# Inverting 16 by 16 triangles in 8 by 8 halves, and issuing their block loads from two engines

## The chip, the cores and the metric

The kernel runs on one core of a Trainium2 chip. The metric is device time in microseconds (us) of one execution; lower is better. Five engines work side by side, each through its own list of instructions in order: TensorE (PE: matmuls and transposes), VectorE (DVE), ScalarE (ACT), GpSimd (POOL) and SyncE (SP, which here only issues DMAs). They wait for one another through semaphores.

## The reference

One gated-DeltaNet layer, then one MoBA attention layer, on 256 tokens of width 1024, float32, 8 heads of 128. What matters here is the first layer's delta rule, in chunks of 64 tokens:

```python
lower = jnp.where(strict, jnp.einsum('nbhid,nbhjd->nbhij', k_beta, k) * decay, 0.0)
a_mat = jnp.eye(C, dtype=jnp.float32) + lower
w = lax.linalg.triangular_solve(a_mat, k_beta * jnp.exp(gc)[..., None],
                                left_side=True, lower=True, unit_diagonal=True)
u = lax.linalg.triangular_solve(a_mat, v * beta[..., None],
                                left_side=True, lower=True, unit_diagonal=True)
```

## The kernel before, in words

The kernel does the same with chunks of 128 tokens (two, t = 0 and 1) and inverts the unit triangular matrix of each head and chunk. The 8 heads make two groups of four; a group has 8 matrices of 128 by 128 (4 heads, 2 chunks). `inverse(grp)` handles one group:

- The 64 diagonal blocks of 16 by 16 (8 matrices, 8 blocks) are fetched from a DRAM copy `md` into tile `inv`, one block in each of 64 partitions. Tile part `mb` is the block (transposed), `t16` the inverse that grows in it, `tr` the pair (inverse, transposed inverse).
- Substitution (lines 742 to 749): 15 steps, each an outer product and an addition over what is left of the block, so 30 instructions. Group 0 does them on POOL, group 1 on DVE (`INVERSE`, line 48).
- SP writes `tr` to the DRAM scratch `td` (752), waits until it has landed, and issues eight small DMAs (755 to 757) that bring it back as blocks on the diagonal of tile `TC`, which is part of tile TR of the group (TR0, TR1). This is the block layout of the change's title.
- PE then doubles the blocks: `ps_x`, `ps_y` (16 to 32), `ps_x5`, `ps_y5` (to 64), `ps_x6`, `ps_y6` (to 128), with copies on DVE and ACT between. `solve` applies the inverse: `ps_s1`, `ps_s2`, `ps_s3`, and `read_out` (`ps_o`, `ps_og`) makes the operand o of the output projection (o0 and o1 for the two groups).

PE is kept busy meanwhile by projections: heads' v (`ps_v`), the gate z (`ps_z`), and the first half of the output projection (`ps_y<-hi,o`, 128x512), which needs o0 alone; its second half needs o1. A v head goes through ACT (copy with a scale), DVE (three steps of a convolution on tile `cv`), ACT again (`cv<-cv`, the silu) and back to PE as a transpose (`ps_vt`). Weights arrive by SP's DMAs as `raw`, are cut into `hi` (ACT) and `lo` (DVE), and a `raw` buffer is loaded again after its `lo`.

The order on every engine is fixed when the program is built. `Clock` estimates when each instruction would run, and `Pipeline` puts a chain's next step after a PE step when the estimate says that its operands are there. In these estimates a DMA issue takes its engine 60 ns (line 172), on SP as on ACT, and a POOL operation on `inv` takes 480 ns and 1.2 ns for each element (199). `ps_x` is put no earlier than 1500 ns after the estimated landing of TC (766). A change in one chain so moves instructions on all engines. Nearly all instructions bear line 220, where they are recorded, so the views are read by tile.

Of the kernel before, what the change touches and what calls it, by code (L numbers as in the profile page):

```python
# [20 lines left out]
ALU = mybir.AluOpType  # L21
# [205 lines left out]
class Pipeline:  # L227
# [12 lines left out]
    def at(self, e):  # L240
        return self.clock.t.get(self.ENGINES[e], START)
# [66 lines left out]
def body(ctx, tc, x, xt, cst_in, w0, wp, a_ln_g, a_ln_b, b_ln_g, b_ln_b, out):  # L308
    ctx.enter_context(tc.manual_schedule())
    nc = Clock(tc.nc)  # L310
# [358 lines left out]
    def gs_head(h):  # L669
# [41 lines left out]
        if n_md[h // 4] == 4:  # L711
            pipe.add(inverse(h // 4), R_INV)
# [8 lines left out]
    def inverse(grp):  # L721
        inv = act.tile([64, 4, 16, 16], F32, tag="ag" if grp == 0 else "ab", name=f"inv{grp}")
        mb, tr, prod = inv[:, 0], inv[:, 1:3], inv[:, 3]
# [7 lines left out]
        TC = T[:, 1024:1536].rearrange("p (w q c) -> p w q c", w=2, q=8)  # L731
        T64 = T[0:64, 1536:2048].rearrange("p (q c) -> p q c", q=8)
        t16 = tr[:, 0]
# [4 lines left out]
                                        ap=[[16 * (P + 1), 64]] + list(blk.ap)))  # L738
        eng, e = INVERSE[grp]
        eng = getattr(nc, eng)  # L740
        yield e, [inv]
        for j in range(15):

            m, r = 15 - j, j + 1
            eng.tensor_mul(prod[:, 0:m, 0:r], mb[:, j, r:16].unsqueeze(2).to_broadcast([64, m, r]),
                           t16[:, j, 0:r].unsqueeze(1).to_broadcast([64, m, r]))
            eng.tensor_add(t16[:, r:16, 0:r], t16[:, r:16, 0:r], prod[:, 0:m, 0:r])
            if j in (4, 9):
                yield e, [t16]
        eng.tensor_copy(tr[:, 1], t16.rearrange("p a b -> p b a"))  # L750
        yield "t", [inv]
        nc.sync.dma_start(td[grp].rearrange("w q b r c -> (q b) w (r c)"),
                          tr.rearrange("p w r c -> p w (r c)"))
        yield "t", [td[grp]]
        for b in range(8):
            nc.sync.dma_start(TC.rearrange("p w q c -> p (w q) c")[16 * b:16 * b + 16, :, 16 * (b % 2):16 * (b % 2) + 16],
                              td[grp].rearrange("w q b r c -> b r (w q) c")[b])

        def ms(q):
# [500 lines left out]
```

## Time and profile before

| | |
|---|---|
| time, median of 3 runs | 301.84 us (301.78 to 303.9) |
| the profiled execution's own time | 302.44 us |
| its span, first to last instruction | 300.5 us |
| PE busy | 289.7 us, 96% |
| DVE, ACT, POOL busy | 210.2, 161.6, 51.2 us |
| mean granted TensorE clock | 0.993 |

The span is what the instructions cover; 1.94 us of the profiled execution lie around it. A window's row gives each engine's busy time in it, so 10 us less PE's figure is what PE stood idle there. A timeline row merges like instructions that follow one another (x10) and gives the idle time of the engine before them, if any, with what ended it.

### The profile page before, as it was taken

What the parts mean: (1) busy time and instruction counts of PE and PEld (TensorE: products, weight loads), DVE (VectorE), ACT (ScalarE), POOL (GpSimd) and SP (SyncE); (2) the same over time, 40 slices, a digit from 0 to 9 for tenths busy, and PEclk for the clock granted to TensorE, in tenths of its full rate; (3) what the DMA queues carried; (4) which work ended last, traced back from release to release, by engine and by line L of the source; (5) the groups of instructions that cost most, each with busy time, mean ns of one, the idle gap of its engine ahead of it and who ended that gap; (6) DMA issues with size and microseconds to landing.
All of it is one profiled execution on the core that took longest, in us unless ns stands there. A gap on an engine that the chain in (4) does not pass through costs nothing.

```text
span 300.5 us, 6569 instructions
## 1 busy us (share of the span) xinstructions
PE 289.7 (96%) x2598; PEld 266.7 (89%) x2598; DVE 210.2 (70%) x477; ACT 161.6 (54%) x329; POOL 51.2 (17%) x92
## 2 busy tenths in 40 slices
PE   8998999999999999999989999999999999999990
PEld 7898989989999989996878888899999999998890
DVE  0699479999999587687449893865655565763545
ACT  2588986635866552865352525775655558561000
POOL 8002310265884300110020010000000000000101
PEclk9999999999999999999999999999999999999997
DMA  6986505659576711336629055895444447400012
GB/s 224 377 278 223 177 17 176 214 165 316 189 258 182 235 61 29 93 127 209 201 108 328 2 179 172 256 313 199 143 129 153 144 143 273 142 0 2 0 70 71
DMA packets 19934, 49.43 MB, mean 164 GB/s; under 512 B 6304, under 2 KB 7968, under 8 KB 19904
## 3 DMA queue, kind: packets, MB, share of 16 engines
q1 hardware_dynamic: 18592, 46.73, 47.3%
q0 software_dynamic: 448, 1.18, 1.4%
q10 hardware_dynamic: 864, 1.11, 1.1%
q8 instruction: 20, 0.33, 0.5%
q14 instruction: 10, 0.08, 0.1%
HBM read 46.65 MB, written 2.36 MB: 163 GB/s over the span
## 4 chain that ended last, share of the span: by engine, by line
PE 77%; ACT 7%; DMA 5%; issue 5%; DVE 4%; ACTq 0%; POOL 0%; POOLq 0%; DVEq 0%; SPq 0%
PE ps_bkq L220 15%; PE ps_y L220 11%; PE ps_kq L220 9%; PE ps_v L220 8%; PE ps_bv L220 7%; PE ps_bz L220 7%; PE ps_z L220 5%; PE ps_g L220 4%; DMA raw<-in_wp_dram 4%; ACT ME L220 3%; DMA zraw<-in_w_dram 2%; PE ps_o L220 2%; PE ps_ot L220 2%; PE ps_sc L220 2%; PE ps_s L220 1%
## 5 line engine op out<-in xcount | busy, mean ns | idle before, releaser
L220 DVE TENSOR_TENSOR lo<-raw,hi 128x1024 fp32r<-128x1024 f32 (+1 forms) x79 | 94.6, 1207 | 10.1 <-ACT hi L220 9.9
L220 ACT CAST hi<-raw 128x1024 fp32r<-128x1024 f32 (+1 forms) x79 | 80.3, 1037 | 12.6 <-DMA raw<-in_wp_dram 6.5
L220 PE MATMUL ps_y<-hi,o 128*128 128x512 f32 (+1 forms) x144 | 43.5, 374 | 0.8 <-ACT o L220 0.7
L220 PE MATMUL ps_bkq<-x1h,hi 128*128 128x256 f32 x128 | 38.0, 297 | 0.0
L220 PE MATMUL ps_kq<-xh,hi 128*128 128x256 f32 x128 | 36.6, 286 | 0.0
L220 PE MATMUL ps_kq<-xh,lo 128*128 128x256 f32 x128 | 35.7, 279 | 0.0
L220 PE MATMUL ps_kq<-xl,hi 128*128 128x256 f32 x128 | 35.6, 278 | 0.0
L220 PE MATMUL ps_bkq<-x1l,hi 128*128 128x256 f32 x128 | 35.6, 278 | 0.0
L220 PE MATMUL ps_bkq<-x1h,lo 128*128 128x256 f32 x128 | 35.5, 278 | 0.0
L220 PEld LDWEIGHTS ps_y<-hi,o 128*128 128x128 f32 x144 | 25.9, 188 | 5.9 <-ACT o L220 1.2
L220 POOL TENSOR_TENSOR mv<-mv,nhalf 128x1 f32<-128x1 f32 x4 | 3.8, 951 | 135.0 <-DVE mv L220 135.0
L220 PE MATMUL ps_y<-lo,o 128*128 128x512 f32 (+1 forms) x72 | 26.3, 366 | 0.0
L220 DVE SCALAR_TENSOR_TENSOR cv<-ps_kq,cst_sb,cv 128x255 f32<-128x255 f32 (+2 forms) x48 | 21.5, 470 | 4.8 <-ACT cv L220 4.6
L220 PEld LDWEIGHTS ps_bkq<-x1h,hi 128*128 128x128 f32 x128 | 24.1, 189 | 0.2
L220 PEld LDWEIGHTS ps_bkq<-x1l,hi 128*128 128x128 f32 x128 | 24.1, 188 | 0.2
L220 PEld LDWEIGHTS ps_kq<-xh,hi 128*128 128x128 f32 x128 | 24.3, 190 | 0.0
L220 PEld LDWEIGHTS ps_kq<-xh,lo 128*128 128x128 f32 x128 | 24.0, 188 | 0.1
L220 PEld LDWEIGHTS ps_kq<-xl,hi 128*128 128x128 f32 x128 | 24.1, 188 | 0.0
L220 PEld LDWEIGHTS ps_bkq<-x1h,lo 128*128 128x128 f32 x128 | 24.1, 188 | 0.0
L220 PE MATMUL ps_v<-xh,hi 128*128 128x256 f32 x64 | 18.7, 292 | 0.0
L220 PE MATMUL ps_bz<-x1h,hi 128*128 128x256 f32 x64 | 18.0, 282 | 0.0
L220 PE MATMUL ps_v<-xl,hi 128*128 128x256 f32 x64 | 17.9, 280 | 0.0
(177 smaller groups left out, 676.6 us busy)
## 6 DMA issues: line engine op xcount, KB each, us to landing
raw<-in_wp_dram SPq DMA_DIRECT2D x77, 512.0 KB, 4.2
md<-ME POOLq DMA_DIRECT2D x8, 128.0 KB, 2.6
late<-in_x_dram SPq DMA_DIRECT2D x1, 1024.0 KB, 4.9
zraw<-in_w_dram ACTq DMA_DIRECT2D x4, 136.0 KB, 4.3
zraw<-in_w_dram ACTq DMA_DIRECT2D x2, 272.0 KB, 4.8
x_sb<-in_xt_dram SPq DMA_DIRECT2D x4, 128.0 KB, 4.1
x_sb<-in_xt_dram SPq DMA_DIRECT2D x2, 256.0 KB, 5.0
raw<-in_wp_dram SPq DMA_DIRECT2D x2, 256.0 KB, 4.1
```

What stands on the lines that cost most here:

```text
L220: r = f(*args, **kw)
```

## The change

The 16 by 16 inverse is made of two 8 by 8 ones. Seven steps of substitution run on both 8-blocks at once (14 instructions of 14 to 32 elements in each partition, where there were 30 of 15 to 64). One merge follows, of two products of three 8 by 8 matrices: each product is one multiplication of 512 elements and a sum over 8, on DVE one reduction, on POOL three additions (256, 128 and 64 elements). The multiplications and reductions are separated by points at which the planner may put other work. Of the eight loads of the block layout, SP issues four and ACT four, ACT's after the same wait for `td`.

```diff
-        for j in range(15):
-            m, r = 15 - j, j + 1
-            eng.tensor_mul(prod[:, 0:m, 0:r], mb[:, j, r:16].unsqueeze(2).to_broadcast([64, m, r]),
-                           t16[:, j, 0:r].unsqueeze(1).to_broadcast([64, m, r]))
-            eng.tensor_add(t16[:, r:16, 0:r], t16[:, r:16, 0:r], prod[:, 0:m, 0:r])
-            if j in (4, 9):
-                yield e, [t16]
+        wide = tr[:, 1]
+        for j in range(7):
+            m, r = 7 - j, j + 1
+            pv = at(wide, 0, 0, (m * r, 2), (r, m), (1, r))
+            tv = at(t16, r, 0, (136, 2), (16, m), (1, r))
+            eng.tensor_mul(pv, at(mb, j, r, (136, 2), (1, m), (0, r)), at(t16, j, 0, (136, 2), (0, m), (1, r)))
+            eng.tensor_add(tv, tv, pv)
+            if j == 3:
                 yield e, [t16]
+        p8 = at(wide, 0, 0, (64, 8), (8, 8), (1, 8))
+        for out, left, right in (...):
+            eng.tensor_mul(p8, left, right)
+            yield e, [inv]
+            if e == "v":
+                eng.tensor_reduce(out, p8, axis=mybir.AxisListType.X, op=ALU.add)
+            else:
+                for w in (4, 2, 1):
...
+                    eng.tensor_add(d, x0, x1)
+            yield e, [inv]
         eng.tensor_copy(tr[:, 1], t16.rearrange("p a b -> p b a"))
...
         for b in range(8):
-            nc.sync.dma_start(TC...[16 * b:16 * b + 16, ...],
+            (nc.scalar if b % 2 else nc.sync).dma_start(TC...[16 * b:16 * b + 16, ...],
```

From the first moved instruction (late in the k and q heads) to the end of the first layer the order differs; from the second layer on PE's order is as before. Three places are shown.

First, ACT while group 0's inverse comes back (cv_1257 before and cv_1260 now are the same head). Before:

```order
L220 ACTIVATE cv_1316<-ps_v_1253,cst_sb_82 128x256
L220 CAST hi31_1319<-raw31_1171 128x1024
L220 ACTIVATE cv_1257<-cv_1257 128x256
L220 ACTIVATE cv_1371<-ps_v_1311,cst_sb_82 128x256
L220 CAST hi32_1373<-raw32_1195 128x1024
```

Now:

```order
L220 ACTIVATE cv_1311<-ps_v_1247,cst_sb_82 128x256
L220 CAST hi31_1314<-raw31_1154 128x1024
L220 DMA TR0_845<-td_174 16x16x16 x4
L220 ACTIVATE cv_1260<-cv_1260 128x256
L220 ACTIVATE cv_1366<-ps_v_1307,cst_sb_82 128x256
L220 CAST hi32_1368<-raw32_1182 128x1024
```

Four DMA issues now stand ahead of the silu of this head; PE's transpose of it comes three projection matmuls earlier than before, and group 0's `ps_x` six.

Second, ACT while group 0 is solved (Z is the solve's result, jk2 the squares of its read-out). Before:

```order
L220 CAST hi36_1706<-raw36_1394 128x1024
L220 ACTIVATE cv_1757<-ps_v_1700,cst_sb_82 128x256
L220 COPY Z_1771<-ps_s1_1773 128x512
L220 ACTIVATE cv_1625<-cv_1625 128x256
L220 ACTIVATE jk2_1820,sso_177<-ps_o_1805 128x128
```

Now:

```order
L220 ACTIVATE W_175<-ps_vt_1748,nk_172 128x128 x2
L220 COPY Z_1751<-ps_s1_1753 128x512
L220 CAST hi37_1771<-raw37_1389 128x1024
L220 DMA TR1_1356<-td_174 16x16x16 x4
L220 ACTIVATE cv_1681<-cv_1681 128x256
L220 ACTIVATE jk2_1803,sso_177<-ps_o_1794 128x128
```

A cast and four DMA issues now stand between the copy of Z and the silu. In both orders PE transposes the head of this silu right after `ps_o`; between `ps_s1` and that transpose it has nine projection matmuls, `ps_s2` and `ps_o`, before and now.

Third, PE between group 1's two read-outs (ps_og are their transposes). Before:

```order
L220 MATMUL ps_og_2275<-ident_121,og_2270 128x128 x4
L220 MATMUL ps_y_2235<-hi35_1627,o0_1772 128x512
L220 MATMUL ps_y_2235<-lo35_1628,o0_1772 128x512
L220 MATMUL ps_y_2235<-hi35_1627,o0_1772 128x512
L220 MATMUL ps_y_2066<-hi36_1706,o1_2208 128x512
```

Now:

```order
L220 MATMUL ps_og_2245<-ident_121,og_2240 128x128 x4
L220 MATMUL ps_y_2258<-hi34_1560,o0_1752 128x512
L220 MATMUL ps_y_2258<-lo34_1561,o0_1752 128x512
L220 MATMUL ps_y_2258<-hi34_1560,o0_1752 128x512 x2
L220 MATMUL ps_y_2258<-lo34_1561,o0_1752 128x512
L220 MATMUL ps_y_2258<-hi34_1560,o0_1752 128x512
L220 MATMUL ps_y_2258<-hi35_1617,o0_1752 128x512
L220 MATMUL ps_y_2258<-lo35_1618,o0_1752 128x512
L220 MATMUL ps_y_2258<-hi35_1617,o0_1752 128x512 x2
L220 MATMUL ps_y_2258<-lo35_1618,o0_1752 128x512
L220 MATMUL ps_y_2258<-hi35_1617,o0_1752 128x512
L220 MATMUL ps_y_2069<-hi36_1683,o1_2169 128x512
```

Before the first matmul that needs o1, PE had three that need only o0; now it has twelve.

## Rows read from the trace of the kernel before

**Rows 1.** The page's first part: busy us, share of span, instructions.
```profile
PE 289.7 (96%) x2598; PEld 266.7 (89%) x2598; DVE 210.2 (70%) x477; ACT 161.6 (54%) x329; POOL 51.2 (17%) x92
```

**Rows 2.** Windows of 10 us: PE, PEld, DVE, ACT, POOL busy, clock, DMA.
```profile
120.00:130.00 10.00, 9.77 (x143) 9.40 (x142) 6.18 (x14) 8.13 (x30) 2.04 (x2) 1.00 0.39 114
130.00:140.00 10.00, 9.62 (x247) 7.63 (x246) 9.62 (x20) 4.95 (x9) 0.00 (x0) 1.00 0.40 129
...
150.00:160.00 10.00, 9.20 (x56) 7.52 (x55) 5.25 (x13) 5.64 (x20) 2.01 (x2) 1.00 0.48 184
...
290.00:300.00 10.00, 3.32 (x30) 3.12 (x28) 4.99 (x12) 0.00 (x0) 0.85 (x1) 0.83 0.15 53
```

**Rows 3.** Waits of PE: us in total, times, longest.
```profile
PE ps_y L220 <- ACT o L220: 0.7, 1, 0.7
PE ps_vt L220 <- ACT cv L220: 0.6, 2, 0.4
```

**Rows 4.** The chain that ended last: start us, us, what.
```profile
81.23 6.80 PE ps_v L220 x60
...
159.33 8.24 PE ps_y L220 x36
```

**Rows 5.** Tile inv: count, ns min/median/max, first and last start, forms.
```profile
L220 POOL TENSOR_TENSOR inv<-inv x30: 212/293/1248, 70.1 to 88.4; 64x15 f32<-64x15 f32 x4, 64x28 f32<-64x28 f32 x4, 64x39 f32<-64x39 f32 x4, 64x48 f32<-64x48 f32 x4
...
L220 POOL COPY inv<-inv x1: 613/613/613, 88.7 to 88.7; 64x256 f32<-64x256 f32 x1
```

**Rows 6.** POOL's groups by shape: busy us, mean ns, idle before.
```profile
L220 POOL TENSOR_TENSOR inv<-inv 64x28 f32<-64x28 f32 x4 | 0.9, 235 | 0.3
...
L220 POOL TENSOR_TENSOR inv<-inv 64x64 f32<-64x64 f32 x2 | 0.6, 299 | 0.2
```

**Rows 7.** Tile lo, 60 to 130 us: DVE's subtraction, as Rows 5.
```profile
L220 DVE TENSOR_TENSOR lo<-raw,hi x20: 1204/1216/1240, 59.2 to 124.9; 128x1024 fp32r<-128x1024 f32 x20
```

**Rows 8.** SP's DMA issues, timeline, 84 to 128 us.
```profile
89.33 0.69 SPq L220 DMA_DIRECT2D td<-inv  x1
...
92.85 4.01 SPq L220 DMA_DIRECT2D TR<-td  x8
...
114.53 0.59 SPq L220 DMA_DIRECT2D td<-inv  x1
116.96 3.77 SPq L220 DMA_DIRECT2D TR<-td  x8
```

**Rows 9.** Timelines of SP and of ACT, 0 to 3.5 us.
```profile
0.81 1.81 SPq L220 DMA_DIRECT2D x_sb<-in_xt_dram  x4
...
0.81 1.85 ACTq L220 DMA_DIRECT2D zraw<-in_w_dram  x4
```

**Rows 10.** Timeline of ACT, around 92 and around 118 us.
```profile
91.78 1.04 ACT L220 CAST hi<-raw 128x1024 fp32r<-128x1024 f32 x1
94.11 0.42 ACT L220 ACTIVATE cv<-cv 128x256 f32<-128x256 f32 x1 [1.29 <-DVE cv L220]
...
117.89 0.59 ACT L220 COPY Z<-ps_s 128x512 f32<-128x512 f32 x1 [1.78 <-PE ps_s L220]
118.38 0.42 ACT L220 ACTIVATE cv<-cv 128x256 f32<-128x256 f32 x1
```

**Rows 11.** Timeline of PE, where the moved steps meet it.
```profile
95.10 0.38 PE L220 MATMUL ps_vt<-ident,cv 128*128 128x128 f32 x2
...
100.80 0.75 PE L220 MATMUL ps_x<-TR,ME 32*32 32x32 f32 x64
...
109.90 1.14 PE L220 MATMUL ps_x<-TR,ME 64*64 64x64 f32 x16
...
120.51 0.38 PE L220 MATMUL ps_vt<-ident,cv 128*128 128x128 f32 x2
```

**Rows 12.** Timeline of DVE, 101 to 121 us.
```profile
104.32 2.24 DVE L220 TENSOR_TENSOR inv<-inv 64x15 f32<-64x15 f32 x10 [0.59 <-DMA inv<-md]
...
108.44 0.87 DVE L220 COPY TR<-ps_y 32x256 f32<-32x256 f32 x2 [0.35 <-PE ps_y L220]
```

More of the change, by code (lines that the diff above doesn't have):

```diff
@@ L741, in inverse, with at @@
         yield e, [inv]
-        for j in range(15):
-            m, r = 15 - j, j + 1
-            eng.tensor_mul(prod[:, 0:m, 0:r], mb[:, j, r:16].unsqueeze(2).to_broadcast([64, m, r]),
-                           t16[:, j, 0:r].unsqueeze(1).to_broadcast([64, m, r]))
-            eng.tensor_add(t16[:, r:16, 0:r], t16[:, r:16, 0:r], prod[:, 0:m, 0:r])
-            if j in (4, 9):
-                yield e, [t16]
+        def at(t, row, col, *dims):
+            return bass.AP(tensor=t.tensor, offset=t.offset + 16 * row + col, ap=[t.ap[0]] + [list(d) for d in dims])
+        wide = tr[:, 1]
[6 more added lines that the diff above has]
+            if j == 3:
+                yield e, [t16]
+        p8 = at(wide, 0, 0, (64, 8), (8, 8), (1, 8))
+        for out, left, right in ((at(mb, 8, 0, (16, 8), (1, 8)), at(mb, 0, 8, (1, 8), (0, 8), (16, 8)),
+                                  at(t16, 0, 0, (0, 8), (1, 8), (16, 8))),
+                                 (at(t16, 8, 0, (16, 8), (1, 8)), at(t16, 8, 8, (16, 8), (0, 8), (1, 8)),
+                                  at(mb, 8, 0, (0, 8), (1, 8), (16, 8)))):
+            eng.tensor_mul(p8, left, right)
[4 more added lines that the diff above has]
+                for w in (4, 2, 1):
+                    d = at(wide, 0, 0, (64, 8), (8, 8), (1, w)) if w > 1 else out
+                    x0, x1 = (at(wide, 0, k, (64, 8), (8, 8), (1, w)) for k in (0, w))
+                    if w == 1:
+                        x0, x1 = (at(wide, 0, k, (64, 8), (8, 8)) for k in (0, 1))
+                    eng.tensor_add(d, x0, x1)
+            yield e, [inv]
         eng.tensor_copy(tr[:, 1], t16.rearrange("p a b -> p b a"))
@@ L755, in inverse @@
         for b in range(8):
-            nc.sync.dma_start(TC.rearrange("p w q c -> p (w q) c")[16 * b:16 * b + 16, :, 16 * (b % 2):16 * (b % 2) + 16],
+            (nc.scalar if b % 2 else nc.sync).dma_start(TC.rearrange("p w q c -> p (w q) c")[16 * b:16 * b + 16, :, 16 * (b % 2):16 * (b % 2) + 16],
                               td[grp].rearrange("w q b r c -> b r (w q) c")[b])
```

## The prediction

> **What bounds the kernel now.** I read the page's busy shares first: PE is busy 289.7 of 300.5 us [rows 1], so only what lets PE stand idle, or makes it stand idle, can move the time. Windows of 10 us show where it does. From 60 us to 290 us PE is full but for three windows, with 0.23, 0.38 and 0.80 us missing, and 6.7 us at the very end [rows 2], where this change moves nothing. The clock was granted in full in the three, so such short waits cost no more than themselves. The waits of PE name them: 0.6 us in two waits of a head's transpose for ACT's silu, 0.7 us of the output projection for group 1's operand o [rows 3]. That is 1.4 us in all (0.23 + 0.38 + 0.80), the most that any better order around the inverse can give. The inverse itself is nowhere on the chain that ended last: PE reaches group 0's `ps_x` at 100.80 without a wait [rows 3, 11], 3.9 us after SP's last load of the block layout was issued (92.85 + 4.01 = 96.86) [rows 8].
>
> **The change, part by part.**
>
> Substitution on POOL (group 0). Before, 30 operations took from 70.1 to 88.7 us. At their median of 293 ns they are 8.8 us of work; most of the rest is operations that took up to 1248 ns [rows 5], as long as one of DVE's `lo` subtractions (1204 to 1240 ns) [rows 7]. An operation costs 235 ns at 28 elements and 299 ns at 64 [rows 6], so 1.8 ns for each further element. The 14 small ones are then 14 x 0.235 = 3.3 us. A merge product is a multiplication of 512 elements (0.30 + 448 x 0.0018 = 1.1 us) and additions of 256, 128 and 64 (0.64 + 0.41 + 0.30): 2.45 us, twice 4.9. Together 8.2 us against 8.8: less than half the instructions, nearly the same work. The waits behind `lo` stay, since DVE's list there holds as many. POOL ends about 0.6 us earlier; I take 0 to 1.5 us, and nobody gains from it: ACT, below, gets to its loads only then.
>
> Substitution on DVE (group 1). Ten steps took 2.24 us [rows 12], so 30 are 6.7 us. Now 14 x 0.22 = 3.1 us, and four operations over 512 elements, at half of a `lo` (0.6 us each) [rows 7], 2.4 us: 1.2 us less. The reduction has no row; between one small step (0.22) and a whole `lo` (1.22) I take the half, since it reads half as many elements. The planner puts convolution steps into the gaps, so `td` leaves SP at about 114.5 as before [rows 8]. PE's order gives DVE one tight place: `ps_x6` needs the first of two copies of `ps_y5`. That copy started at 108.44 (0.43 us each) [rows 12] and `ps_x6` at 109.90 [rows 11], so 1.0 us to spare. Ahead of the copies now stand 14 small steps, one product and a `lo` where ten steps stood: 3.1 + 0.6 + 1.2 - 2.2 = 2.7 us more. By the order, 60 projection matmuls instead of 42 lie between `ps_x` and `ps_x6`; at 0.113 us (6.80 / 60) [rows 4] PE comes 2.0 us later, less 0.3 us for reaching `ps_x` earlier. That leaves 1.0 + 1.7 - 2.7 = 0. I take 0, at worst 0.8.
>
> SP's half of the loads. Eight issues took 4.01 and 3.77 us [rows 8], so SP is free some 1.9 us sooner for weights. PE never waits for weights there [rows 3]: worth 0, hidden by the projections' own lead.
>
> ACT's half, the part that costs. ACT's only DMA issues so far, at the start, took 1.85 us for four [rows 9]; SP's loads of the layout give the same, 3.77 / 2 = 1.89 [rows 8]. The planner counts 60 ns each. So each group's issues hold up ACT's list by 1.85 us, of which 0.24 is planned. Group 0: `hi` runs from 91.78 for 1.04 us, the issues to 92.8 + 1.85 = 94.65, the silu behind them (0.42) to 95.1 [rows 10]. PE's transpose of that head stood at 95.10 [rows 11] and now comes three matmuls, 0.34 us, earlier: PE waits 0.3 us. Most of the issues fall into the 1.29 us that ACT stood idle there [rows 10]. Group 1 has no such gap. Before, the silu started 0.49 us after the copy of Z did (118.38 - 117.89) [rows 10], and PE's transpose came 2.62 us after that start (120.51) [rows 11]. Now 0.49 + 1.04 (`hi`) + 1.85 + 0.42 = 3.80 us pass: 1.2 us late, 1.1 with instructions overlapping by 0.1. Bounds for the pair: 0, if the issues overlap ACT's work; 1.4 + 2 x 1.85 = 5.1, if the two queues hinder each other so that each issue takes twice as long. I take 1.4, since the rows of both queues lie at 0.46 to 0.47 us an issue.
>
> [...]
>
> What the new order takes away. Group 1's o: PE had three matmuls to do before it, now twelve; nine more at 0.229 us (8.24 / 36) [rows 4] are 2.06 us, over the 0.80 us of idle time: -0.8. The transpose behind the 0.38 us wait now comes before the doubling, and the one behind 0.23 us stands just after PE's new wait, which gives ACT the time: -0.6.
>
> Sum: -1.4 + 0.3 + 1.1 + 0.2 (new waits of 0.1 us, as `ps_x5` now follows a short transposition only) = +0.2 us. The profiled execution took 302.44 us, its span and 1.94 around it: 302.6 now. The median of the runs shown is 0.6 lower: **302.0 us**.
>
> **The rivals.**
>
> *ACT's issues cost next to nothing.* For it: no row shows ACT issuing while one of its operations runs, so an overlap is not excluded, and group 0's gap hides most anyway. Against: nothing else of ACT's fell between its issues at the start, and they still took 1.85 us [rows 9]. Without the 1.4 us: 300.6.
>
> *ACT parks on `td`.* In-order ACT waits for `td` to land before its issues, with silu, casts and read-out queued behind and PE behind those. There is no slack: the first load could go at 92.85 [rows 8], and ACT arrives at 92.8. Each us that POOL ends later than before (89.3, the end of its copy) [rows 5] is a us of PE. For it: no row has a POOL operation of two inputs over 64 elements, and `lo` may stop a long one. Against: the slope above has POOL end slightly earlier. It makes the kernel slower by 1% from 2.9 us on, when a merge product costs 4.2 us instead of 2.45 and the 0.6 is used up; at 3 us the time is 305.0.
>
> *Two queues hinder each other.* Both now issue the same loads at once. If each issue takes twice as long, PE's two waits grow by 1.85 each: 305.7. For it: these loads are many short pieces, those at the start long rows. Against: at the start SP and ACT issued four each at the same time in 1.81 and 1.85 us [rows 9]. [...]
>
> **How the numbers follow.** The forecast has 0.64, cheap issues 0.18, parking 0.09, hindrance 0.06, anything else 0.03. 1%, about what a measurement of this kernel can tell from no change, lies at 298.8 and 304.9. Faster by more needs over 3.0 us, where all of PE's waits are 1.4: 0.02. Slower by more holds most of hindrance, half of parking: 0.10. Within 1%: 0.88. The range runs from cheap issues (300.6, with 0.1 for scatter) to the forecast with 0.8 at `ps_x6` and POOL 1 us late: 302.0 + 1.8 = 303.8.
>
> **What would show it.** In the changed profile: PE's idle time at 155 us gone; a wait of `ps_vt` for `cv` of about 1.1 us near 120 us and one of 0.3 near 95; four ACT issues of TR in about 1.85 us, twice; POOL's 14 + 8 operations on `inv` ending between 87 and 89; the 512-element multiplication at 1.1 us on POOL, 0.6 on DVE. The prediction is wrong if ACT waits for `td`, if PE waits for TR at `ps_x`, or if ACT's issues show no wait of PE behind them.

## The result: slower by 1.3%, from two gaps of TensorE

| | before | after |
|---|---|---|
| median of 17 runs each (us) | 301.50 | 305.90 |
| lowest and highest (us) | 300.96, 303.90 | 303.62, 312.90 |
| profiled execution, its span (us) | 302.44, 300.5 | 306.14, 304.4 |

The ratio is 1.013, with a 95% interval from 1.011 to 1.015; like every ratio below it leaves out executions over 1.5% above the fastest of their kernel (two of the changed kernel's, 310.81 and 312.90 us), so it is a little under 305.90 / 301.50. The forecast was 302.0 us and its range ended at 303.8; the time lies above both.

The page of the changed kernel, first part (busy us, share of the span, instructions), answers to [rows 1]:

```profile
PE 290.9 (96%) x2598; PEld 268.4 (88%) x2598; DVE 213.2 (70%) x465; ACT 162.1 (53%) x329; POOL 53.4 (18%) x84
```

POOL has 8 instructions fewer and is busy 2.2 us longer. PE's waits from 80 to 160 us (total, times, longest) answer to [rows 3]:

```profile
PE ps_g L220 <- ACT kq L220: 2.3, 1, 2.3
PE ps_y L220 <- issue: 1.7, 1, 1.7
PE ps_vt L220 <- ACT cv L220: 0.2, 1, 0.2
```

Of the three waits of before, the one for o and the longer one for cv are gone; the one of 0.23 us for cv is still there. Two new ones, which I had not foreseen, are longer than all the old ones. The windows of the changed kernel, with columns as in [rows 2] (the second is the window's length), the last two against the rows there:

```profile
20.00:60.00 40.00, 39.82 (x308) 36.86 (x308) 33.99 (x94) 31.93 (x73) 9.21 (x13) 1.00 0.51 167
...
85.00:90.00 5.00, 2.75 (x18) 2.02 (x16) 4.96 (x9) 0.83 (x2) 3.73 (x6) 1.00 0.61 200
100.00:105.00 5.00, 4.38 (x141) 3.97 (x139) 0.69 (x2) 2.89 (x6) 1.96 (x4) 1.00 0.69 229
105.00:107.00 2.00, 0.96 (x78) 0.93 (x79) 0.99 (x6) 0.48 (x2) 0.00 (x0) 1.00 0.00 0
107.00:111.00 4.00, 4.00 (x48) 3.71 (x49) 3.72 (x14) 0.60 (x2) 0.00 (x0) 0.57 0.34 101
...
130.00:140.00 10.00, 9.74 (x280) 8.83 (x279) 6.66 (x14) 6.45 (x19) 1.01 (x1) 1.00 0.60 233
150.00:160.00 10.00, 10.00 (x68) 9.07 (x67) 5.40 (x12) 6.19 (x21) 2.93 (x2) 1.00 0.46 147
```

This makes up the 3.9 us between the two spans: +2.25 for the gap before `ps_g`, +1.66 for the gap inside the small matmuls of `ps_y`, +1.7 for the four microseconds behind it at a granted clock of 0.57 (4.0 x 0.43, an estimate; from 107.76 to 109.47 us a projection matmul of `ps_v` starts every 0.21 us, where 0.113 is usual [rows 4]). Against that stand -1.41 for the old gaps, +0.49 for what is left (the old one of 0.23, and two new ones of 0.13), and about -0.6 before 60 us, where PE's order is still that of before (38.98 us of PE in 20 to 60 before, 39.82 here, and a new stop of 0.2 at 16 us). The sum is 4.1. It holds for these two executions; the others have no trace.

**The first gap starts on POOL.** POOL's groups by shape, 60 to 95 us (busy us, mean ns | idle before), answer to [rows 6]:

```profile
L220 POOL TENSOR_TENSOR inv<-inv 64x512 f32<-64x512 f32 x2 | 4.7, 2334 | 0.2
...
L220 POOL TENSOR_TENSOR inv<-inv 64x64 f32<-64x64 f32 x2 | 0.6, 295 | 0.2
```

The second of the two products in POOL's timeline (start, us):

```profile
83.48 2.55 POOL L220 TENSOR_TENSOR inv<-inv 64x512 f32<-64x512 f32 x1
```

DVE's timeline in that time:

```profile
77.05 1.51 DVE L220 SCALAR_TENSOR_TENSOR cv<-ps_kq,cst_sb,cv 128x255 f32<-128x255 f32 x3
78.48 2.61 DVE L220 TENSOR_TENSOR lo<-raw,hi 128x1024 fp32r<-128x1024 f32 x1
...
83.43 1.20 DVE L220 TENSOR_TENSOR lo<-raw,hi 128x1024 fp32r<-128x1024 f32 x1
84.55 1.49 DVE L220 SCALAR_TENSOR_TENSOR cneg<-cneg,beta 128x2 f32<-128x2 f32 x1
```

The last of these in the kernel before:

```profile
83.22 0.17 DVE L220 SCALAR_TENSOR_TENSOR cneg<-cneg,beta 128x2 f32<-128x2 f32 x1
```

The first product runs from 77.88 to 80.00 us, 2.12 us instead of the 1.1 of my sum. The `lo` that DVE starts at 78.48 takes 2.61 us instead of 1.22 [rows 7] and ends 1.09 us after the product. The second product is held up by a `lo` for about 1.1 us of its 2.55, and then holds up `cneg`, two elements wide: 1.49 us instead of 0.17, done 0.02 us after the product. That is 1.39 + 1.32 = 2.7 us of DVE's time. The convolution steps, which read one operand from PSUM, took their usual 0.5 us each beside the first product (1.51 us for the three; the page's mean over all 48 is 0.47). What DVE brings late, ACT and PE wait for. ACT's timeline, with the idle time ahead and what ended it in brackets:

```profile
87.97 0.42 ACT L220 ACTIVATE kq<-cv 128x256 f32<-128x256 f32 x1 [3.39 <-DVE cv L220]
```

PE's timeline:

```profile
88.43 1.13 PE L220 MATMUL ps_g<-kq 128*128 128x512 f32 x2 [2.25 <-ACT kq L220]
```

PE's new order has a share in this gap, which I had overlooked. In the trace of before, 634 matmuls stand ahead of this `ps_g`; in those of the kernels with the new steps on POOL there are 625 (e9 to e11 have their added ones besides). The planner has moved nine projection matmuls behind it, 1.0 us at 0.113 us each [rows 4], so PE gets to `ps_g` 1.0 us earlier. The order alone makes no gap: e2 below has it too, and PE waits 0.07 us there. But with the old order an estimate from these rows leaves 2.25 - 1.0 = 1.2 us of the gap; no run tried it.

**ACT's issues cost next to nothing.** ACT around group 1's loads, with its issues as "ACTq":

```profile
122.14 0.59 ACT L220 COPY Z<-ps_s 128x512 f32<-128x512 f32 x1 [0.21 <-PE ps_s L220]
122.20 0.31 ACTq L220 DMA_DIRECT2D TR<-td  x1
122.62 1.05 ACT L220 CAST hi<-raw 128x1024 fp32r<-128x1024 f32 x1
122.82 1.32 ACTq L220 DMA_DIRECT2D TR<-td  x3
124.25 0.42 ACT L220 ACTIVATE cv<-cv 128x256 f32<-128x256 f32 x1 [0.57 <-DVE lo L220]
```

An issue takes 0.31 to 0.49 us, near what I had read from [rows 8, 9], but three of the four ran while the copy and the cast were running. Only 0.47 us, from the cast's end (123.67) to the last issue's (124.15), stand alone before the silu. What stands behind the issues does wait for them: the silu starts 0.10 us after the last one ends. It is done at 124.67 us, 0.10 before PE transposes this head (124.77), so PE is spared by a small margin. The third rival, two queues that hinder each other, isn't seen either: where both issue at once, at 94 us, SP's issues take 0.34 and 0.45 us and ACT's 0.34 and 0.47, no longer than one queue's alone, and PE never waits for TR at `ps_x`.

### The profile page after: what moved, and what is told of

It is laid out like the page before. It is cut to its first block, busy times and chain, and to the rows that moved or that the text cites. A ratio compares the mean times of both kernels' runs of the same rounds, so it can differ in the third digit from the quotient of the medians.

```text
span 304.4 us, 6557 instructions
## 1 busy us (share of the span) xinstructions
PE 290.9 (96%) x2598; PEld 268.4 (88%) x2598; DVE 213.2 (70%) x465; ACT 162.1 (53%) x329; POOL 53.4 (18%) x84
## 4 chain that ended last, share of the span: by engine, by line
PE 80%; DVE 6%; issue 6%; DMA 4%; ACT 2%; ACTq 0%; POOL 0%; POOLq 0%; DVEq 0%; SPq 0%
PE ps_bkq L220 15%; PE ps_y L220 13%; PE ps_kq L220 11%; PE ps_bv L220 7%; PE ps_bz L220 7%; PE ps_v L220 6%; PE ps_z L220 5%; PE ps_g L220 4%; DVE lo L220 3%; DMA zraw<-in_w_dram 2%; PE ps_o L220 2%; PE ps_ot L220 2%; DMA raw<-in_wp_dram 2%; PE ps_sc L220 2%; PE ps_s L220 1%
## 5 line engine op out<-in xcount | busy, mean ns | idle before, releaser
L220 DVE TENSOR_TENSOR lo<-raw,hi 128x1024 fp32r<-128x1024 f32 (+1 forms) x79 | 96.6, 1230 | 11.0 <-ACT hi L220 10.9
L220 PE MATMUL ps_v<-xh,lo 128*128 128x256 f32 x64 | 18.3, 287 | 0.0
```

Source lines behind the costliest of these rows:

```text
L220: r = f(*args, **kw)
```

## The experiments

Each ran against the kernel before on the same chip. Ratios are given with their 95% intervals. Where TensorE's gaps are given, they are from the trace.

**1. The merge on POOL alone, the merge on DVE alone.** The one keeps the 15 steps in group 1, the other in group 0:

```diff
+        if grp == 1:        # e7 ("grp == 0" in e1, e1b, e1c)
+            ... the 15 steps of before
+        else:
             ... the 8-blocks and the merge
```

e7_pool_new_only, with all loads from SP: 

> The kernel before with the merge on GpSimd (group 0) alone; VectorE keeps the 15 steps, and SyncE issues all loads. Theory A: the gap of 2.3 us near 86 us is there, and the 1.4 us of group 1's old gaps stay: 304.5 to 307 us, as slow as the whole change or slower. Rival B (the merge on VectorE costs the time): 301 to 302.

Measured: 304.63 us, ratio 1.0093 (1.0074 to 1.0112). The first gap is there, the second is small:

```profile
PE ps_g L220 <- ACT kq L220: 2.4, 1, 2.4
PE ps_y L220 <- issue: 0.3, 1, 0.3
```

POOL's merge alone makes the kernel slower. Except for the 0.2 us for cv the old gaps are gone here too, and in e1b below, where only group 1 is new, they are gone as well. So either new order removes them, without the other group's merge; that part of the expectation was wrong. In this execution the clock falls behind the first gap, too; it is 0.66 in these five microseconds:

```profile
88.00:93.00 5.00, 4.55 (x18) 3.52 (x19) 4.96 (x13) 2.53 (x5) 0.55 (x1) 0.66 0.66 213
```

That is 5.0 x 0.34 = 1.7 us more. In the changed kernel's trace the clock stays at 1.00 behind its gap of 2.25 us, so the same gap can cost 2.3 us or 4; what decides it is not shown.

e1_pool_old: 

> Group 0 on GpSimd goes back to the 15 steps of before; group 1 on VectorE keeps the merge, and the loads stay on ScalarE and SyncE in turn. Theory A (the two 512-element products of GpSimd, 2.12 and 1.42 us in the changed kernel, keep VectorE's SBUF operations waiting: lo took 2.61 us for 1.21, cneg 1.49 for 0.17): TensorE's gap of 2.26 us at 86.2 us is gone, and the time falls by that at least, to 303.6 us or less; with the gap of 1.66 us at 104.4 and the lower clock behind it gone too, to 300.5 (the 1.4 us that group 1's new place wins stays). Rival B (ScalarE's loads and the merge on VectorE cost the time): still 305 to 306. Rival C (the gap at 104.4 us has a cause of its own): 303.6, with the gap still there.

Measured: 300.63 us, ratio 0.9978 (0.9955 to 1.0001). Its profiled execution took 1640.86 us, with TensorE busy for 1630.8 of them, and is left aside; why is not known. It ran a second time for its trace, as e1b_pool_old: 

> The kernel of the first of these runs once more (15 steps on GpSimd, merge on VectorE, loads in turn), for its trace and a narrower interval. Theory A: no gap at 86 or 104 us, the three old gaps of TensorE (1.4 us) mostly gone, 300.0 to 301.2 us, 0.2 to 0.5% under the kernel before. Rival: 301.6, no difference.

Measured: 301.73 us, ratio 0.9993 (0.9973 to 1.0012). In its trace both new gaps are gone; 0.3 us of the second kind are left, and the cv wait of 0.2:

```profile
PE ps_y L220 <- issue: 0.3, 1, 0.3
PE ps_vt L220 <- ACT cv L220: 0.2, 1, 0.2
```

e1c_pool_old_sp: 

> The kernel before with the merge on VectorE (group 1) alone; GpSimd keeps the 15 steps and SyncE issues all loads. Theory: no gap at 86 us; the old gaps of TensorE at 139 and 155 us gone: 300 to 301.5 us, at or just under the kernel before. Rival (part of the time lost comes with the merge on VectorE): 303 or more.

Measured: 303.30 us, ratio 1.0029 (1.0002 to 1.0056). The executions run from 299.80 to 308.59 us; their median meets the rival's 303, while the ratio stands for 302.4, between the two. The profiled execution is the one of 308.59 us. It has no gap at `ps_g`, but three of the second kind, and a granted clock of 0.54 from 137 to 152 us:

```profile
PE ps_y L220 <- issue: 2.0, 2, 1.5
PE ps_v L220 <- issue: 0.4, 1, 0.4
```

So the second gap needs neither the merge on POOL nor the first gap. The merge belongs on DVE, if anywhere; no version with it beats the kernel before by more than the measurement is uncertain.

**2. The loads alone.** e3 is the changed kernel with all loads from SP, e4 the kernel before with the loads in turn (the one line of the change):

```diff
-            (nc.scalar if b % 2 else nc.sync).dma_start(TC...   # e3
+            r = tc.nc.sync.dma_start(TC...
+            nc.note(...)    # the planner still counts four of them on ACT, so the order stays
```

e3_sp_loads: 

> The changed kernel with all eight loads of the block layout issued by SyncE, and the order of every engine's other work as in the changed kernel. My prediction's step (four issues hold ScalarE's list for 1.85 us, worth 0.3 + 1.1 us): 1.4 us less than the changed kernel, 304.5. Rival (issues run beside ScalarE's operations, as the trace of the changed kernel shows a cast running across them): the same as the changed kernel within 0.5 us, about 305.9, with both TensorE gaps at 86 and 104 us unchanged.

e4_loads_only: 

> The kernel before with only the loads of the block layout issued by ScalarE and SyncE in turn; the substitution is the old one. If issues run beside ScalarE's operations: the time of before, 301.5 us, within 0.5. If four issues hold ScalarE's list for 1.85 us: 1.0 to 1.5 us more, with TensorE waiting for a transpose of cv near 95 or 120 us.

Measured: e3 306.15 us, ratio 1.0146 (1.0106 to 1.0186), with gaps of 2.5 and 1.3 us; e4 301.88 us, ratio 1.0017 (1.0002 to 1.0032), with the three old gaps of TensorE unchanged. The rival that issues cost next to nothing is right: e4's interval leaves them at most 1 us, and e3 shows no gain from taking them away, where 1.4 us were expected. In e3 the clock stays at 1.00 behind both gaps.

**3. The same products, cut in eight.** Everything else stands in the changed kernel's order:

```diff
-            eng.tensor_mul(p8, left, right)
...                                            # VectorE (group 1) as before
+                for i in range(8):
+                    tc.nc.gpsimd.tensor_mul(p8[:, i:i + 1, :], left[:, i:i + 1, :], right[:, i:i + 1, :])
...                                            # the planner still counts one product
```

e2_pool_cut8: 

> The changed kernel with each of GpSimd's two 512-element products issued as eight products of 64 elements; the order of every engine's other work is that of the changed kernel. Theory A1 (the length of one operation, since a VectorE operation waits for the end of the GpSimd operation that is running): VectorE's lo beside the products stays below 1.6 us, TensorE's gap at 86 us is gone or under 0.3 us although GpSimd works as long (8 x 0.3 = 2.4 us a product): 303.6 us or less, 300.5 if the gap at 104 goes too. Rival A2 (GpSimd's traffic as such slows VectorE, or GpSimd's lateness counts): gap and time stay, 305 to 306. Rival D (the order in which the planner now puts ps_g ahead of other work makes the gap): the gap stays.

Measured: 307.65 us, ratio 1.0199 (1.0172 to 1.0227): slower still. Theory A1 holds for the first gap, which shrinks to 0.07 us, and the longest `lo` beside the products takes 1.45 us. But the sixteen pieces take 10.5 us, because five of them wait for a `lo` (1.21 to 1.42 us each, where the others take 0.34 to 0.43). POOL's copy ends at 93.4 us instead of 88.3, and `td` is written late. SP's timeline:

```profile
93.42 0.68 SPq L221 DMA_DIRECT2D td<-inv  x1
```

ACT's timeline:

```profile
96.43 1.89 ACTq L221 DMA_DIRECT2D TR<-td  x4
98.42 0.42 ACT L221 ACTIVATE cv<-cv 128x256 f32<-128x256 f32 x1 [6.46 <-issue]
```

PE's waits, 80 to 160 us:

```profile
PE ps_vt L221 <- ACT cv L221: 5.1, 2, 4.8
```

ACT waits for `td` with the silu behind it. This is the second rival of the prediction, at 4.8 us; the changed kernel itself does not show it, since its POOL ends in time.

e5_cut8_sp: 

> The kernel with the products cut in eight (307.7 us, where TensorE stood idle for 4.84 us at 94 us behind a transpose of cv) with all loads of the block layout issued by SyncE; the order of every engine's other work is kept. Theory (ScalarE's four loads waited for td, since GpSimd ended its copy at 93.4 us instead of 88.3, and silu stood behind them): the gap at 94 us is gone, and the time falls by 4 us or more, to 301 to 303.6 us; TensorE may wait at ps_x instead, at most 2 us. Rival (cv is late for another reason, VectorE's list for one): the gap at 94 us stays and the time is within 1 us of 307.7. On the gap at 104 us: if it follows from the stall at 86 us, it stays away.

Measured: 306.63 us, ratio 1.0155 (1.0128 to 1.0182). The wait at 94 us falls from 4.8 to 0.6 us, so its cause is shown. The time did not follow: PE now waits 0.7 us for the loads at `ps_x` and 1.9 us in two gaps of the second kind, which by my expectation would stay away if they followed from the stall at 86 us; that stall is down to 0.6 us here.

**4. The same products in another layout.** The sum index moves from the innermost to the middle dimension of the product, so the innermost operand is contiguous or repeated instead of 16 elements apart, and the additions run over contiguous pieces. The operands of the first product, as (step, count) of each dimension:

```diff
-  p8[i,j,k]: left (1,8),(0,8),(16,8)   right (0,8),(1,8),(16,8)
+  p8[i,k,j]: left (1,8),(16,8),(0,8)   right (0,8),(16,8),(1,8)
```

e6_layout: 

> The changed kernel with GpSimd's two 512-element products in another order of their output (row, sum index, column): the innermost operand is now contiguous or repeated, as in the old 15 steps, and the additions run over contiguous pieces. Same operations, same sizes, same order on every engine. Theory L (the stride of the operands made the product cost 2.12 and 1.42 us where I had put 1.1): both take 1.0 to 1.3 us, lo and cneg behind them wait 0.4 to 1.0 us less each, TensorE's gap at 86 us shrinks from 2.26 to about 0.5 to 1.3 us, the time to 303.5 to 305. Rival S (the size alone makes the cost): products and time as in the changed kernel, about 306.

Measured: 302.65 us, ratio 1.0025 (1.0005 to 1.0045): most of the loss is gone. Its profiled execution, too, is one of 1640 us (1641.54). Once more for its trace, as e6b_layout: 

> The kernel with GpSimd's products in the contiguous layout once more, for its trace (its time was 302.7 us, 3.3 under the changed kernel's 305.9). Theory L: products of 1.0 to 1.3 us; VectorE's lo and cneg behind them wait 0.4 to 1.0 us less; TensorE's gap at 86 us is down from 2.26 us to 0.5 to 1.3, and the gap of 1.66 us at 104 us is gone, since the time fell by more than the first gap can give. Rival: the products are as long as before and the gain lies elsewhere.

Measured: 302.91 us, ratio 1.0057 (1.0036 to 1.0078). POOL's products, by shape:

```profile
L220 POOL TENSOR_TENSOR inv<-inv 64x512 f32<-64x512 f32 x2 | 3.2, 1613 | 0.2
```

DVE's timeline:

```profile
77.80 1.63 DVE L220 TENSOR_TENSOR lo<-raw,hi 128x1024 fp32r<-128x1024 f32 x1
...
82.96 1.04 DVE L220 SCALAR_TENSOR_TENSOR cneg<-cneg,beta 128x2 f32<-128x2 f32 x1
```

PE's waits, 80 to 160 us:

```profile
PE ps_y L220 <- issue: 1.6, 1, 1.6
PE ps_g L220 <- ACT kq L220: 0.9, 1, 0.9
```

The first product takes 1.15 us, where nothing holds it; the second 2.08 with 0.9 us behind a `lo`. So the 1.1 us of the prediction is right for this layout, and the stride of 16 elements (64 bytes) in both operands made it 2.12 us. The first gap follows it: 2.25 to 0.91 us. The expectation that the second gap goes too was wrong: this execution has it, at 1.6 us. The medians fall by 3.0 us (305.90 to 302.91), the first gap gives 1.34 of that; what else the executions without a trace have less is not shown. The product with both operands strided takes 85% more (2.12 against 1.15).

e8_layout_both, DVE's product and reduction in that layout too: 

> The same with VectorE's two products (group 1) in that layout too, its reductions reading with a stride of 8. If the stride also made VectorE's product cost 1.06 us (I had put 0.6), the product takes 0.6 to 0.8 us; the reduction (0.67 us) stays or grows. Group 1's chain then ends up to 0.8 us earlier, but no wait of TensorE hangs on it: 302.2 to 302.9 us either way. Rival (VectorE's cost is by size alone): product 1.06 us again.

Measured: 305.02 us, ratio 1.0100 (1.0058 to 1.0142), above the expectation; the profiled execution took 302.5 us, with gaps of 0.6 and 0.3. DVE's groups by shape, 100 to 120 us, in the changed kernel:

```profile
L220 DVE TENSOR_TENSOR inv<-inv 64x512 f32<-64x512 f32 x2 | 2.1, 1062 | 0.1
L220 DVE TENSOR_REDUCE inv<-inv 64x64 f32<-64x512 f32 x2 | 1.3, 673 | 0.0
```

And here:

```profile
L220 DVE TENSOR_REDUCE inv<-inv 64x64 f32<-64x512 f32 x2 | 2.1, 1060 | 0.0
L220 DVE TENSOR_TENSOR inv<-inv 64x512 f32<-64x512 f32 x2 | 1.4, 684 | 0.1
```

The strided reading cost 0.4 us in either place: moved from the product to the reduction, it changes their sum by nothing (1.74 us each way). Why this kernel's other executions were slower than e6b's stays open.

**5. The second gap.** It lies inside 128 small matmuls, and no event of the program ends it. DMA's queues in the changed kernel, from 96 to 103.6 us (packets, MB, share):

```profile
q1 hardware_dynamic: 1485, 1.52, 61.9%
q10 hardware_dynamic: 1087, 0.07, 9.7%
q0 software_dynamic: 57, 0.17, 7.6%
q14 instruction: 1, 0.01, 0.3%
```

The same view from 103 to 106 us has a queue more:

```profile
q8 instruction: 1, 0.02, 2.0%
```

A 16-KB packet of instructions arrives around TensorE's stop (it lasts from 103.70 to 104.66, PE stops at 104.38 and goes on at 106.04). I take queue q8 for that of TensorE's instructions: 20 packets of 16 KB, one for every 260 or so of its 5,196 matmuls and weight loads.

What I had not counted says more. With the 47 other records of TensorE's list (mostly semaphore instructions) counted in, the gap comes behind record 1,729. The traces of all kernels together (without the two of 1640 us) have 15 waits of PE that are put down to "issue", in twelve of them, and each comes behind record 1,729, 1,985, 2,753 or 3,009: 256, 1,024 and 1,280 later than the first, all whole multiples of 256, and 256 is near what one packet holds by the counts (5,243 records in 20 packets, 262 each). Every one of them ends 1.26 to 1.53 us after the end of a 16-KB packet. Fourteen lie within the small matmuls; one, of 0.4 us in e1c, lies between two projection matmuls.

In the kernel before, the packet that belongs here came at 98.47, at record 1,451, 278 records ahead of the place. In the traces of after, e3, e6b and e7, which have the gap there, it came only at record 1,587 to 1,629, as the weight loads' traffic ended. Four kernels shift the packets against the program:

```diff
+    for _ in range(16):     # 32, 48
+        tc.nc.tensor.matmul(ps_warm[0:32, 0:32], ones[0:32, 0:32], ones[0:32, 0:32], start=True, stop=True)
     keep_warm(WARM)
```

e9_shift64: 

> The changed kernel with 16 small matmuls (64 instructions) more at TensorE's start, where it waits for its first data; they change no result and no other order. Theory F (the second gap is TensorE waiting for its own instructions, which come in packets of 16 KB): the packets fall 64 instructions earlier in the program, the gap moves, shrinks or goes, and the time changes by up to 3 us from 305.9, down to 303.0 if gap and low clock go. Rival (the gap comes from data or from the stall at 86 us): gap and time as before, 305.9 within 0.6, and all three shifts alike.

e10_shift128: 

> The same with 32 small matmuls (128 instructions). Theory F: another time than the unshifted kernel's, 303 to 308 us, with the gap at another place or gone; the gap at 86 us stays at 2.2 to 2.5 us. Rival: 305.9 within 0.6.

e11_shift192: 

> The same with 48 small matmuls (192 instructions). Theory F: another time again, 303 to 308 us, the gap at 86 us unchanged. Rival: 305.9 within 0.6.

e12_before128: 

> The kernel before with 32 small matmuls (128 instructions) more at TensorE's start. Theory F: it has the same bursts of small matmuls, so it too can lose 1 to 3 us when a packet comes late: 301.5 to 304.5 us, with a gap in ps_x or ps_y that nothing of the program ends where the time is over 302.5. Rival: 301.5 within 0.4.

Measured: 306.66, 310.07, 312.86 and 310.24 us, ratios 1.0125 (1.0079 to 1.0172), 1.0252 (1.0212 to 1.0291), 1.0328 (1.0280 to 1.0376) and 1.0265 (1.0231 to 1.0298). They are not clean: the added matmuls ran slower than I had thought, and TensorE's z projection starts at 6.97, 8.67, 10.09 and 8.52 us instead of 5.1 to 5.3. So up to 1.7, 3.4, 4.8 and 3.4 us of the times are this late start. What the traces show apart from it: at 64 the gap is absent from this burst, and one of 0.3 us stands in group 1's `ps_x` (the profiled execution took 303.48 us, the other five 305.2 to 309.3); it is 0.97 us at 128 and 1.37 at 192. The gap at `ps_g` is 1.8, 2.4 and 2.5 us, and at 128 the clock falls behind it (0.66 from 90 to 95 us). The kernel before, whose trace does not have it, has it when shifted by 128. PE's waits there, 80 to 160 us:

```profile
PE ps_y L220 <- issue: 2.8, 1, 2.8
```

Its windows:

```profile
100.00:105.00 5.00, 4.82 (x198) 4.37 (x197) 2.21 (x4) 3.31 (x6) 1.25 (x4) 1.00 0.94 333
105.00:107.00 2.00, 0.00 (x0) 0.00 (x0) 0.91 (x5) 0.00 (x0) 0.00 (x0) 1.00 0.63 217
107.00:116.00 9.00, 8.37 (x130) 7.75 (x131) 3.58 (x14) 2.84 (x6) 0.00 (x0) 0.62 0.04 14
```

Its DMA queues, 104.9 to 107 us:

```profile
q8 instruction: 1, 0.02, 3.5%
```

It loses 2.8 us there and 3.4 us more (9.0 x 0.38) at the lower clock behind. Only the added matmuls and their late start distinguish it from the kernel before.

The count is what speaks against a cause in the program: e10, e11 and e12 have their gap behind record 1,985 all three, although their shifts put other instructions of the program there, and although e12 and e1c have no stall at `ps_g`. So I read the second gap as TensorE out of instructions: in both kernels it stands at places 256 records or multiples of that apart, and a 16-KB packet comes 1.26 to 1.53 us ahead of its end. No row of a trace names that cause. What holds a packet back is not shown: a start 3.4 us late also moves the weight loads, so the place of the packets and that of the loads were not separated. One execution of e9 with almost no such gap beside five slower ones suggests that it also varies from execution to execution, and with it the spread of after (303.6 to 312.9 us); without their traces that is not shown.

## Why the prediction was wrong

- **Removing PE's three waits, -1.4 us: right for two of them** (0.38 and 0.80 us, with two new ones of 0.13 in their stead, 0.2 foreseen). The third, 0.23 us, stays: PE's new wait of 1.1 us ahead of it, which was to give ACT the time, didn't come. Either new order alone removes the two (e7, e1b).
- **POOL's product at 1.1 us: wrong, and the step that failed.** "A merge product is a multiplication of 512 elements (0.30 + 448 x 0.0018 = 1.1 us)" took its slope from operands that are contiguous or repeated in the innermost dimension. The new operands are 16 elements apart, both in the first product, one in the second: 2.12 us and about 1.4. In the old layout it is 1.15 (e6b), so the slope was sound and its use was not.
- **The step that was missing:** a long operation of POOL held up DVE (a `lo` of 2.61 us for 1.22 beside the product of 2.12). I had read only the other direction, POOL's 1248 ns behind a `lo` [rows 5], and priced POOL as if only its own end mattered ("nobody gains from it"). DVE was busy almost throughout and PE had no slack behind it. With the nine matmuls that the new order takes from ahead of `ps_g` (1.0 us, which I had not looked at either), this costs 2.25 us of PE, more than everything the new order gives. It was no rival of mine. Cutting the products (e2) and shortening them (e6b) both shrink that gap; with the product at 1.15 us 0.91 of it is left, so the wrong size alone does not explain it.
- **ACT's issues, +0.3 and +1.1 us: wrong.** They ran beside the ACT operations that stand ahead of them (three of group 1's four beside a copy of 0.59 us and a cast of 1.05); e4 leaves them at most 1 us, and e3 finds no gain without them. My reason, "the rows of both queues lie at 0.46 to 0.47 us an issue", was right about an issue and not about what it holds up. The first rival had it, at a chance of 0.18.
- **ACT parking on `td`:** did not happen, because POOL ended at 88.3 us, a microsecond sooner than before. The forecast of 0.6 sooner is right by accident: POOL began 0.8 us sooner (69.3 us for 70.1) and took as long as before, 19.0 us for 19.2, so the smaller count of instructions gave nothing. e2 shows the rival at work.
- **DVE's product 0.6, reduction 0.6 us:** 1.06 and 0.67. The same stride, worth 0.4 us in the product; no wait of PE hangs on it, and none stands at `ps_x6`, as forecast.
- **Not seen at all:** the second gap and the clock behind it, 3.4 us of the profiled execution. Nothing in the trace of before shows such a gap. That TensorE can stop within its small matmuls for an instruction packet, as I read the gap, could not be told from a busy share; e12 shows that the program before can have it too. So even with the first gap priced right the forecast would have been short by this much.

## What to carry to other kernels

Fewer instructions on GpSimd are no gain by themselves (here its substitution took 19.0 us with 22 operations and 19.2 with 30): look up what VectorE does in the meantime, since here a long GpSimd operation (2.12 us) kept VectorE's operations on two SBUF tensors back (2.61 us for 1.22), and short ones waited out theirs (1.21 to 1.42 us for 0.34 to 0.43). Price an operation by rows with the same innermost stride, not by element count alone (2.12 us against 1.15 for the same 512 elements). And where a burst of very small matmuls runs while weights are loading, compare the instruction queue's packets with the burst, and count the instructions ahead of each unexplained gap, before blaming the order: here all such gaps lay whole multiples of 256 apart, and no wait of the program did.

## What the runs showed of the hardware

- GpSimd and VectorE's operations on two SBUF tensors held each other up in both directions: a `lo` at 2.61 us behind a product of 2.12 (1.22 alone), a two-element operation at 1.49 us (0.17 alone), and GpSimd's 64-element pieces at 1.21 to 1.42 us behind a `lo` (e2), against 0.34 to 0.43 alone. VectorE's convolution steps on a PSUM tensor took 0.5 us beside the product as elsewhere.
- An innermost stride of 64 bytes: GpSimd's 512-element product 2.12 us against 1.15 with both operands strided; VectorE's 1.06 against 0.68, and its reduction, at 32 bytes, 1.06 against 0.67.
- ScalarE's DMA issues of 0.31 to 0.49 us ran while its own earlier copy (0.59 us) or cast (1.05) ran; in group 1 the silu behind them started 0.10 us after the last.
- TensorE stood idle, with nothing of the program to wait for, in gaps of 0.3 to 2.8 us, nearly all in bursts of 32x32 matmuls, at whole multiples of 256 records from one another, each ending 1.26 to 1.53 us after a 16-KB instruction packet. That it was out of instructions is my reading of these figures.
- A lower granted clock stands behind the four longest of these gaps, of 1.5 to 2.8 us: 0.57 for 4 us (after), 0.66 for 5 (e6b), 0.62 for 9 (e12), 0.54 for 15 (e1c). Behind e3's, of 1.3 us, it stays at 1.00, and in e5, whose gaps are 1.0 us at most, it is 0.86 and 0.80 in the two windows from 100 to 110 us.
